# The token axis of a two-layer trunk kernel: 304 columns in the order meta, sample, prompt, and 288 where the meta tokens are dropped

## The chip, the cores and the metric

The kernel runs on one core of one Trainium2 chip. The metric is device microseconds of one execution, as the median of several runs. The engines of the core work side by side and in their own order: TensorE (PE, with its weight loads as PEld), VectorE (DVE), ScalarE (ACT), GpSimd (POOL) and SyncE (SP), which issues most DMAs.

## What is computed

One step of a trunk of two layers, for a prompt group (256 tokens, with 16 meta tokens ahead of them) and a sample group (8 sequences of 4 tokens) with the same weights. Layer 0 mixes with RWKV-7, layer 1 with Mamba-2; after each comes a PEER mixer, in which every token picks 16 of 16384 experts in each of 8 heads. The model width is 1024. The reference, cut:

```python
hp = concatenate([meta, x_prompt], axis=1)              # 16 + 256 tokens
yp, ... = trunk(hp, zeros..., lead_pad=M_CHUNK - N_META, chunk=M_CHUNK)
ys, ... = trunk(x_sample, states..., 0, x_sample.shape[1])
return (yp[:, N_META:], ys, ...)                        # states too

def trunk(h, ...):
    for i in range(DEPTH):                               # DEPTH = 2
        xn = rms_norm(h, norm_mix[i])
        out = rwkv7_time_mix(xn, ...) if i % 2 == 0 else mamba2_mix(xn, ...)
        h = h + out
        h = h + peer_ffn(rms_norm(h, norm_ffn[i]), ...)
    return rms_norm(h, norm_final), ...

# rwkv7, per head, one step of the scan
S = S * w_t + (S @ -kk_t) (kk_t * a_t)^T + v_t k_t^T
o_t = S @ r_t
# mamba2
zxbcdt = xn @ in_proj                                    # gate z, conv input x/B/C, dt
xbc = silu(conv_b + sum(full[:, j:j + L] * conv_w[j] for j in range(4)))   # causal, over tokens
y = ssd(...) + d_skip * xs                               # chunked state-space scan
yg = y * silu(z); yg = yg * rsqrt(mean(yg * yg) + eps) * norm_w            # per group of 512
out = yg @ out_proj
# peer
s = q . sub_keys; top 16 of 128 on both sides, then top 16 of their sums
out = sum over experts of gate * gelu(x . u_e) * v_e
```

The output of the meta tokens is not returned. They reach the prompt through the two mixers alone (the RWKV state, the conv and the Mamba state), so behind Mamba's projections nothing needs their columns any more.

## The kernel before

**Layout.** The residual `h` is held transposed: 128 partitions, 8 blocks of channels, and along the row the tokens, `T = 320` columns: 32 sample tokens, 16 meta tokens, 16 columns of zeros, 256 prompt tokens (`prep`). All elementwise work and most products have this token axis as their row, so they are 320 columns wide.

**Products.** `mm3` (L302, L303, L305) multiplies in three passes, for 8 blocks of the contraction: the weight's high part by the activation's high part (L302) and low part (L303), then the weight's low part by the high part (L305). That is 24 matmuls for one block of 128 output channels. The weights come by DMA as `wraw` (L287), ACT rounds them into `whi` (L276), and DVE or POOL makes `wlo` (L283, L281). Smaller products stay in plain fp32, which the trace shows as two instructions each.

**Stages, in order of time.**

- *RWKV front* (`rwkv`, 0 to 97 us): norm; the shifted difference `dx` (L378 to L383; POOL writes the columns where a sequence begins and clears the empty ones); LoRA products (L407, L408, L431, L432); then eight blocks of the key product `pk` by `mm3` with the gates (L451 to L458) between them.
- *RWKV heads* (`rwkv_heads`, 97 to 390 us): eight pairs of heads, each a generator, started nine ticks apart and advanced in turn. Each projects r and v (L607, fp32, 320 columns), scans the decay, and then works on five groups of 64 columns (`u` 0 to 4): group 0 holds samples, meta and the empty columns, groups 1 to 4 the prompt. Masks (`const_masks`) separate the sequences. The output is copied by one ACT instruction (L806), and the sample states are put in at the end (L811 to L835).
- *W_o* (390 to 426 us): eight blocks by `mm3` into `po`, added to `h`.
- *PEER 0* (`peer(0, 3)`, 426 to 1345 us): 16 query blocks `pq` by `mm3` (L892 evacuates them on DVE); scores of 64 + 128 + 128 tokens; the selection of the experts on DVE (`topk`), while PE begins with the first scan (`s_chunk`: 128 chunks of `psc`, 256 prompt columns each); one-hot products (L1120); and the second scan over the value table (L1273, `acc`), with the rest of the first scan woven in. The prompt goes through these dense scans; the samples and meta tokens are gathered row by row (L1051, L1148), in `ng = 3` groups of 16 columns.
- *Mamba* (`mamba`, 1345 to 1743 us): norm; 41 projection blocks `pi` by `mm3`: dt (block 40), 24 conv blocks (`conv`), 16 gate blocks z. A conv block is copied by ACT into `cst` (L1368 the samples, L1369 the rest); POOL fills in the old rows of the conv state, zeros, and a halo of three columns (L1370), which carries the last meta tokens across the empty columns to the prompt; ACT and three DVE instructions convolve (L1374, L1376), ACT applies Silu (L1379, L1381). Then per group of heads the state-space scan (`ssd`), the norm of the group (`pv`, L1581) and the output product `pout` (L1641 adds it to `h`).
- *PEER 1* (`peer(1, 2)`, 1743 to 2674 us): as PEER 0, but only samples and prompt are gathered and scanned; the query blocks still have all 320 columns. The final norm is at its end.

**Order.** Within a stage the order of the instructions on each engine is laid out when the kernel is built, by a planner that goes by priorities in the order of the code; in the two PEER stages (`tc.block(schedule_with_timeline_sim=True)`) it goes by a timeline of estimated durations as well. `keep_in_program_order` and `manual_schedule` fix some places by hand. DMAs of weights go through SP's queue, the gathers and the state outputs through POOL's.

Of the kernel before, what the change touches and what calls it, by code (L numbers as in the profile page):

```python
# [34 lines left out]
T = 320  # L35
D = 1024
# [34 lines left out]
def const_masks():  # L71
# [5 lines left out]
    chunk0 = np.where(t < 32, t // 4, np.where(t < 48, 100, 200 + t))  # L77
# [25 lines left out]
    for kb in range(8):  # L103
# [31 lines left out]
    c["sel0"] = ((np.where(p < 96, q, 32 + q))[:, None] == np.arange(64)[None, :]).astype(np.float32)  # L135
# [12 lines left out]
           "cr": ["mar", "ml1", "ml1t", "mx", "eye64", "blk", "hc", "hb", "rs", "mb", "mbq"],  # L148
# [77 lines left out]
class K:  # L226
    def __init__(self, ctx, tc, a, o):
# [9 lines left out]
        self.h = self.cp.tile([128, KB, T], F32, name="h")  # L237
# [103 lines left out]
    def rwkv(self):  # L341
# [34 lines left out]
        def shifted(k):  # L376

            V.scalar_tensor_tensor(xn[:, k], self.h[:, k], self.vec("nm0", k), ri, op0=ALU.mult, op1=ALU.mult)  # L378
            V.tensor_sub(dx[:, k, 1:], xn[:, k, :T - 1], xn[:, k, 1:])
# [94 lines left out]
        P.tensor_copy(sho[:, :, 0:8], xn[:, :, 3:32:4])  # L474
# [18 lines left out]
        def sm2(name, shape=(128, T), dt=F32):  # L493
            n = int(np.prod(shape[1:]))
            return sp.tile(list(shape), dt, name=name, tag=f"s{n}", bufs=SMB[n])
# [94 lines left out]
    def rwkv_heads(self, kb, xr, xv, kr, sgw, aa, inv2, oo, bv, sm, cm):  # L590
# [44 lines left out]
        for lo, hi, n in ((0, 32, 4), (32, 64, 16), (64, T, 64)):  # L635
# [10 lines left out]
        nc.gpsimd.tensor_copy(lamE[:, 0:8], lam[:, 3:32:4])  # L646
        nc.gpsimd.tensor_copy(lamE[:, 8:12], lam[:, 127:T:64])
# [13 lines left out]
        kEt = sm("kEt"); vt = sm("vt")  # L661
        kEt, vt = u5(kEt), u5(vt)
# [13 lines left out]
        pa5 = pab[:, 0:T].rearrange("p (u c) -> p u c", c=64)  # L676
        for u in U:
            ts = slice(u * 64, (u + 1) * 64)
            for hs in HS:
                mm(pab[hs, T:448] if u == 0 else pb4[hs, u - 1], lhsT=bh[hs, ts], rhs=ar[hs, :, ts], start=True, stop=True)  # L680
                mm(pa5[hs, u], lhsT=ar[hs, 0, ts], rhs=bh[hs, ts], start=True, stop=True)
        V.tensor_mul(X3[:, 0, 64:192], pab[:, T:448], mar[:, 0])
        V.tensor_mul(X3[:, 1:5, 64:192], pb4, mar[:, 1:2].to_broadcast([128, 4, 128]))
        Tm = u5(sm("Tm"))
        V.tensor_mul(Tm[:, 0], pa5[:, 0], C["ml1"][:, 0])
        V.tensor_mul(Tm[:, 1:5], pa5[:, 1:5], C["ml1"][:, 1:2].to_broadcast([128, 4, 64]))
        AT = u5(sm("AT"))
# [5 lines left out]
        for u in U:  # L693
            ts = slice(u * 64, (u + 1) * 64)
# [5 lines left out]
        TT = u5(sm("TT"))  # L700
        V.tensor_mul(TT, AT, C["ml1t"][:, None, :].to_broadcast([128, 5, 64]))
        TF = u5(sm("TF"))
        for li, sz in enumerate((2, 4, 8, 16, 32)):
# [8 lines left out]
            Xs = u5(sm("Xs"))  # L712
# [48 lines left out]
        nc.scalar.copy(QP[:, 0:32], pu0[:, 1, 0:32])  # L761
# [15 lines left out]
        V.tensor_add(QP[:, 32:64], pq0[:, 0:32], ar[:, 1, 0:32])  # L777
        V.tensor_add(QT, pq4[:, :, 64:128], u5(ar[:, 1, 64:T]))
# [27 lines left out]
        nc.scalar.copy(o, po.rearrange("p u c -> p (u c)"))  # L806
# [893 lines left out]
```

## Time and profile before

| what | value |
|---|---|
| median of 3 runs | 2676.23 us (2675.41 to 2686.91) |
| the profiled execution | 2676.22 us, span 2674.4 us |
| mean granted clock of TensorE | 0.977 |
| idle-free stages of PE | 97 to 390 us and 795 to 1320 us: 290.0 of 293 and 518.0 of 525 us busy |
| stretches with little PE work | 610 to 650 us (15.8 of 40 us), 1345 to 1420 us (50.9 of 75 us) |
| HBM traffic | 440.90 MB read, 16.69 MB written |

How such a page is read: the span runs from the first instruction to the last of one execution; what lies around it (1.8 us here) is not in the trace. An engine's busy share is a mean over stages that have different limits, so the windows view, which gives the busy time of each engine in a stretch, says more: where one engine fills a stretch, work taken off it shortens the stretch, and where none does, the waits say what each engine waited for. A matmul's shown duration holds the time until its result is out, and the next one starts before that; the time from start to start is what a matmul costs in a dense run of them.

### The profile page before, as it was taken

What the parts mean: (1) busy time and instruction counts of PE and PEld (TensorE: products, weight loads), DVE (VectorE), ACT (ScalarE), POOL (GpSimd) and SP (SyncE); (2) the same over time, 40 slices, a digit from 0 to 9 for tenths busy, and PEclk for the clock granted to TensorE, in tenths of its full rate; (3) what the DMA queues carried; (4) which work ended last, traced back from release to release, by engine and by line L of the source; (5) the groups of instructions that cost most, each with busy time, mean ns of one, the idle gap of its engine ahead of it and who ended that gap; (6) DMA issues with size and microseconds to landing.
All of it is one profiled execution on the core that took longest, in us unless ns stands there. A gap on an engine that the chain in (4) does not pass through costs nothing. (4 is left out here: it accounts for less than half of the span.)

```text
span 2674.4 us, 47364 instructions
## 1 busy us (share of the span) xinstructions
PE 2506.7 (94%) x18281; PEld 2156.3 (81%) x18281; DVE 1912.9 (72%) x3713; ACT 1246.7 (47%) x2324; POOL 1012.7 (38%) x895
## 2 busy tenths in 40 slices
PE   7999999996989999999978888999979899999998
PEld 4677769996978888888765776899979788888886
DVE  5355556897695777788784787769949856776777
ACT  3322233453784444444454543335448744444444
POOL 4111110485980233424146455106959501122220
PEclk9999999998999999999999999999989999999999
DMA  3111115453417788888732443454633267788784
GB/s 148 52 46 44 41 58 174 138 179 105 136 42 213 255 304 303 299 301 311 256 93 87 146 154 124 129 181 148 184 110 114 62 217 250 259 279 260 262 270 156
DMA packets 125858, 460.68 MB, mean 172 GB/s; under 512 B 14816, under 2 KB 15744, under 8 KB 122432
## 3 DMA queue, kind: packets, MB, share of 16 engines
q1 hardware_dynamic: 99488, 361.08, 42.0%
q0 software_dynamic: 26144, 96.56, 10.1%
q8 instruction: 144, 2.36, 0.4%
q14 instruction: 82, 0.67, 0.1%
HBM read 440.90 MB, written 16.69 MB: 171 GB/s over the span
## 5 line engine op out<-in xcount | busy, mean ns | idle before, releaser
L276 ACT CAST whi<-wraw 128x1024 fp32r<-128x1024 f32 (+1 forms) x619 | 641.9, 1038 | 892.0 <-PE acc L1273 283.5
L283 DVE TENSOR_TENSOR wlo<-wraw,whi 128x1024 fp32r<-128x1024 f32 (+1 forms) x493 | 601.2, 1220 | 423.8 <-ACT whi L276 326.9
L302 PE MATMUL psc<-xh,whi 128*128 128x256 f32 x2048 | 509.0, 285 | 4.6 <-ACT h L1065 2.6
L303 PE MATMUL psc<-xl,whi 128*128 128x256 f32 x2048 | 507.0, 284 | 0.0
L281 POOL TENSOR_TENSOR wlo<-wraw,whi 128x1024 fp32r<-128x1024 f32 (+1 forms) x150 | 357.5, 2390 | 181.3 <-PE pq L305 72.5
L302 PEld LDWEIGHTS psc<-xh,whi 128*128 128x128 f32 x2048 | 392.8, 192 | 12.0 <-ACT whi L276 3.0
L303 PEld LDWEIGHTS psc<-xl,whi 128*128 128x128 f32 x2048 | 392.9, 192 | 5.6
L305 PE MATMUL psc<-xh,wlo 128*128 128x256 f32 x2048 | 291.6, 284 | 0.3 <-POOL wlo L281 0.3
L1051 POOL DMA_INDIRECT G<-in_un,gi x80 | 112.1, 1401 | 472.6 <-DVE glo L283 308.9
L1273 PE MATMUL acc<-whi,glo 128*128 128x512 f32 x1024 | 284.4, 398 | 6.7 <-DVE glo L283 6.7
L1273 PE MATMUL acc<-whi,gh 128*128 128x512 f32 x1024 | 284.6, 398 | 4.4 <-ACT whi L276 3.3
L1273 PE MATMUL acc<-wlo,gh 128*128 128x512 f32 x1024 | 281.8, 396 | 0.0
L305 PEld LDWEIGHTS psc<-xh,wlo 128*128 128x128 f32 x2048 | 265.2, 192 | 1.2 <-POOL wlo L281 0.7
L1273 PEld LDWEIGHTS acc<-whi,glo 128*128 128x128 f32 x1024 | 193.3, 189 | 54.6 <-DVE glo L283 7.6
L1148 POOL DMA_INDIRECT G<-in_v,gi x80 | 120.1, 1502 | 302.7 <-DVE G L1143 165.7
L1273 PEld LDWEIGHTS acc<-wlo,gh 128*128 128x128 f32 x1024 | 192.7, 189 | 47.8 <-DVE wlo L283 1.3
L1273 PEld LDWEIGHTS acc<-whi,gh 128*128 128x128 f32 x1024 | 184.0, 189 | 44.8 <-ACT whi L276 6.5
L1120 PE MATMUL pwt<-ob,oa 128*128 128x128 f32 x1024 | 144.7, 281 | 11.6 <-DVE ob L1094 8.0
L1120 PEld LDWEIGHTS pwt<-ob,oa 128*128 128x128 f32 x1024 | 127.7, 191 | 23.1 <-issue 19.2
L302 PE MATMUL pi<-xh,whi 128*128 128x320 f32 x328 | 107.0, 337 | 13.1 <-ACT cst L1369 4.7
L303 PE MATMUL pi<-xl,whi 128*128 128x320 f32 x328 | 105.8, 334 | 4.1 <-DVE xl L336 3.8
L283 DVE TENSOR_TENSOR glo<-G,gh 128x256 fp32r<-128x256 f32 x256 | 106.7, 418 | 2.7 <-ACT gh L276 2.7
(485 smaller groups left out, 4462.4 us busy)
## 6 DMA issues: line engine op xcount, KB each, us to landing
wraw<-in_u SPq DMA_DIRECT2D x256, 512.0 KB
wraw<-in_v SPq DMA_DIRECT2D x256, 512.0 KB
wraw<-in_win SPq DMA_DIRECT2D x41, 512.0 KB
wraw<-in_wq SPq DMA_DIRECT2D x32, 512.0 KB
wraw<-in_rkv SPq DMA_DIRECT2D x24, 512.0 KB
h<-in_ssm SPq DMA_DIRECT2D x8, 1024.0 KB
out_sssm<-h POOLq DMA_DIRECT2D x8, 1024.0 KB, 4.7
wraw<-in_wo SPq DMA_DIRECT2D x8, 512.0 KB
```

Source lines behind the costliest of these rows:

```text
L276: self.nc.scalar.copy(hi, x)
L281: self.nc.gpsimd.tensor_sub(lo[:, :n], x[:, :n], hi[:, :n].bitcast(F32))
L283: self.nc.vector.tensor_sub(lo[:, n:], x[:, n:], hi[:, n:].bitcast(F32))
L302: nc.tensor.matmul(ps, lhsT=whi[:, k], rhs=xhi[:, x0 + k], start=start and k == 0, stop=False)
L303: nc.tensor.matmul(ps, lhsT=whi[:, k], rhs=xlo[:, x0 + k], start=False, stop=False)
L305: nc.tensor.matmul(ps, lhsT=wlo[:, k], rhs=xhi[:, x0 + k], start=False, stop=stop and k == kb - 1)
L1051: nc.gpsimd.indirect_dma_start(out=rows, out_offset=None, in_=a[f"un{l}"], in_offset=bass.IndirectOffsetOnAxis(ap=gi[:, 0, g, m:m + 1], ax ...
L1120: mm(pw[:, j], lhsT=oa[:, j], rhs=ob[:, j], start=True, stop=True)
L1148: nc.gpsimd.indirect_dma_start(out=rows, out_offset=None, in_=vrows, in_offset=bass.IndirectOffsetOnAxis(ap=gi[:, 1, g, m:m + 1], axis=0))
L1273: mm(acc[i], lhsT=g[:, t0:t0 + 128], rhs=w[:, d0:d0 + 512], start=b == 0 and g is gh and w is vhf, stop=b == 127 and w is vlf)
```

## The change

The token axis has 304 columns: 16 meta tokens, 32 sample tokens, 256 prompt tokens, with no empty columns. So the meta tokens can be dropped by starting a view at column 16, and what is left is contiguous.

- All of RWKV, the PEER 0 queries, and Mamba's dt and conv blocks take 304 columns.
- Mamba's gate blocks, gate, group norm and output product, and the PEER 1 queries take 288 (`M0`, `TM`, `C0`).
- Heads: the five groups stay 64 wide; group 0 is columns 0 to 63, and so holds the first 16 prompt tokens too, which its masks leave out; groups 1 to 4 begin at column 48. The output copy becomes two instructions, the add into `QP` two.
- Conv: meta and prompt now follow each other in `cst`, so POOL's halo copy is gone; the copy out of PSUM has three pieces in place of two, the Silu of the second part two in place of one, and the convolution has 328 columns in place of 344.
- The shifted difference needs no clearing of empty columns. The first scan reads the prompt from column 48 of rows of 304, before from column 64 of rows of 320. `h` keeps its 2560 columns of memory (`hp`), because PEER uses it as scratch.

The diff, cut to its core (the masks and index changes that only follow the new order are left out):

```diff
-T = 320
+T = 304
+TP = 320
...
-    x = np.concatenate([I["x_sample"].reshape(32, D), I["meta_tokens"], np.zeros((16, D), np.float32),
-                        I["x_prompt"].reshape(256, D)], axis=0)
+    x = np.concatenate([I["meta_tokens"], I["x_sample"].reshape(32, D), I["x_prompt"].reshape(256, D)], axis=0)
...
-        self.h = self.cp.tile([128, KB, T], F32, name="h")
+        self.hp = self.cp.tile([128, KB * TP], F32, name="h")
+        self.h = self.hp[:, 0:KB * T].rearrange("p (k t) -> p k t", t=T)
...
-            P.tensor_sub(dx[:, k, 0:32:4], shift[:, k], xn[:, k, 0:32:4])
-            P.tensor_scalar(dx[:, k, 32:33], xn[:, k, 32:33], -1.0, None, op0=ALU.mult)
-            P.memset(dx[:, k, 48:64], 0.0)
-            P.tensor_sub(dx[:, k, 64:65], xn[:, k, 47:48], xn[:, k, 64:65])
+            P.tensor_scalar(dx[:, k, 0:1], xn[:, k, 0:1], -1.0, None, op0=ALU.mult)
+            P.tensor_sub(dx[:, k, 16:48:4], shift[:, k], xn[:, k, 16:48:4])
+            P.tensor_sub(dx[:, k, 48:49], xn[:, k, 15:16], xn[:, k, 48:49])
...
+        us_ = lambda u: slice(0, 64) if u == 0 else slice(64 * u - 16, 64 * u + 48)
...
-            ts = slice(u * 64, (u + 1) * 64)
+            ts = us_(u)
...
-        V.tensor_add(QP[:, 32:64], pq0[:, 0:32], ar[:, 1, 0:32])
+        V.tensor_add(QP[:, 48:64], pq0[:, 16:32], ar[:, 1, 16:32])
+        V.tensor_add(QP[:, 0:16], pq0[:, 32:48], ar[:, 1, 32:48])
...
-        nc.scalar.copy(o, po.rearrange("p u c -> p (u c)"))
+        pof = po.rearrange("p u c -> p (u c)")
+        nc.scalar.copy(o[:, 0:48], pof[:, 0:48])
+        nc.scalar.copy(o[:, 48:T], pof[:, 64:320])
...
+        C0 = 48 - 16 * ng
...
-            pq = self.bank([128, T], "pq", "so"[i % 2])
-            self.mm3(pq, w, (xh, xl))
+            pq = self.bank([128, T - C0], "pq", "so"[i % 2])
+            self.mm3(pq, w, (xh[:, :, C0:], xl[:, :, C0:]))
...
-        TS = ((0, 64), (64, 192), (192, 320))
+        TS = ((C0, C0 + 64), (48, 176), (176, 304))
...
-            self.mm3(p, w, (xh[:, :, 64:T], xl[:, :, 64:T]))
+            self.mm3(p, w, (xh[:, :, 48:T], xl[:, :, 48:T]))
...
-        hs = self.h.rearrange("p k t -> p (k t)")
+        hs = self.hp
...
+        M0 = 16
+        TM = T - M0
...
-            p = self.bank([128, T], "pi", "i" if done[0] % NU < 2 or done[0] >= NU else "f")
+            c0 = M0 if blk < 16 else 0
+            p = self.bank([128, T - c0], "pi", "i" if done[0] % NU < 2 or done[0] >= NU else "f")
...
-            self.mm3(p, w, (xh, xl))
+            self.mm3(p, w, (xh[:, :, c0:], xl[:, :, c0:]))
...
-            if done[0] <= NU:
-                V.tensor_mul(s8[:, :, 3:7], p[:, 0:32].rearrange("p (b t) -> p b t", t=4), ri[:, 0:32].rearrange("p (b t) -> p b t", t=4))
-                V.tensor_mul(s[:, 59:347], p[:, 32:320], ri[:, 32:320])
-            else:
-                nc.scalar.copy(s8[:, :, 3:7], p[:, 0:32].rearrange("p (b t) -> p b t", t=4))
-                nc.scalar.copy(s[:, 59:347], p[:, 32:320])
-            P.tensor_copy(s[:, 88:91], s[:, 72:75])
+            for dst, src in ((s8[:, :, 3:7], slice(16, 48)), (s[:, 59:75], slice(0, 16)), (s[:, 75:331], slice(48, T))):
+                f = (lambda t: t.rearrange("p (b t) -> p b t", t=4)) if src.start == 16 else lambda t: t
+                if done[0] <= NU:
+                    V.tensor_mul(dst, f(p[:, src]), f(ri[:, src]))
+                else:
+                    nc.scalar.copy(dst, f(p[:, src]))
...
-            nc.scalar.activation(ac, s[:, 0:344], AF.Identity, bias=self.vec("cb", blk), scale=self.vec("cw", blk))
+            nc.scalar.activation(ac, s[:, 0:328], AF.Identity, bias=self.vec("cb", blk), scale=self.vec("cw", blk))
...
-            nc.scalar.activation(r[:, 96:384], ac[:, 56:344], AF.Silu)
+            nc.scalar.activation(r[:, 96:128], ac[:, 56:88], AF.Silu)
+            nc.scalar.activation(r[:, 128:384], ac[:, 72:328], AF.Silu)
...
-            pv = self.bank([128, T], "pv", "t")
+            pv = self.bank([128, TM], "pv", "t")
...
-            zs = gp.tile([128, 4, T], F32, name="zs", tag="zs")
+            zs = gp.tile([128, 4, TM], F32, name="zs", tag="zs")
...
-            p = self.bank([128, T], "pout", "i")
+            p = self.bank([128, TM], "pout", "i")
...
-            V.tensor_add(self.h[:, m], self.h[:, m], p)
+            V.tensor_add(self.h[:, m, M0:], self.h[:, m, M0:], p)
```

More of the change, by code (lines that the diff above doesn't have):

```diff
@@ L76, in const_masks @@
     t = np.arange(64)
-    chunk0 = np.where(t < 32, t // 4, np.where(t < 48, 100, 200 + t))
+    chunk0 = np.where(t < 16, 100, np.where(t < 48, t // 4, 200 + t))
     mar = np.zeros((128, 2, 2, 64), np.float32)
@@ L134, in const_masks @@
     c["rs3"] = rs3
-    c["sel0"] = ((np.where(p < 96, q, 32 + q))[:, None] == np.arange(64)[None, :]).astype(np.float32)
+    c["sel0"] = ((p[:, None] < 96) & (q[:, None] == np.arange(32)[None, :])).astype(np.float32)
     c["bmask"] = (q[:, None] // 4 == np.arange(8)[None, :]).astype(np.float32)
@@ L494, in sm2 @@
             n = int(np.prod(shape[1:]))
-            return sp.tile(list(shape), dt, name=name, tag=f"s{n}", bufs=SMB[n])
+            w = n // T * TP if n % T == 0 else n
+            t = sp.tile([128, w], dt, name=name, tag=f"s{w}", bufs=SMB[w])[:, 0:n]
+            return t if len(shape) == 2 else t.rearrange("p (a b) -> p a b", b=shape[2])
         self.psum(r=1, A=2, L=2, c=2, s=1)
@@ L595, in tr, with sm5 @@
         def tr(pt, src, u, hs):
-            mm(pt[hs, u], lhsT=src[hs, u * 64:(u + 1) * 64], rhs=C["eye"][hs, hs], start=True, stop=True)
+            mm(pt[hs, u], lhsT=src[hs, us_(u)], rhs=C["eye"][hs, hs], start=True, stop=True)
         def u5(t):
             return t.rearrange("p (u c) -> p u c", c=64)
+        us_ = lambda u: slice(0, 64) if u == 0 else slice(64 * u - 16, 64 * u + 48)
+        def sm5(name):
+            return u5(sm(name, (128, 320)))
         v = sm("v")
@@ L634, in rwkv_heads @@
         dE = sm("dE")
-        for lo, hi, n in ((0, 32, 4), (32, 64, 16), (64, T, 64)):
+        for lo, hi, n in ((0, 16, 16), (16, 48, 4), (48, T, 64)):
             cv = cs[:, lo:hi].rearrange("p (c n) -> p c n", n=n)
@@ L760, in rwkv_heads @@
         nc.scalar.copy(PU[:, 0], pu0[:, 0])
-        nc.scalar.copy(QP[:, 0:32], pu0[:, 1, 0:32])
+        nc.scalar.copy(QP[:, 16:48], pu0[:, 1, 16:48])
         nc.scalar.copy(PU[:, 1:5], pu4)
@@ L819, in rwkv_heads @@
         for hs in HS:
-            mm(pst[hs], lhsT=PX[hs], rhs=C["eye64"][hs, 32:64], start=True, stop=True)
-        V.tensor_add(o[:, 0:32], o[:, 0:32], pst)
+            mm(pst[hs], lhsT=PX[hs], rhs=C["sq"][hs], start=True, stop=True)
+        V.tensor_add(o[:, 16:48], o[:, 16:48], pst)
         yield
@@ L891, in peer @@
         for i in range(16):
-            V.tensor_mul(qT[:, i], pq.pop() if i == 0 else query(i), ri)
+            V.tensor_mul(qT[:, i, C0:], pq.pop() if i == 0 else query(i), ri[:, C0:])
         for k in range(KB):
@@ L898, in peer @@
             for k in range(4):
-                mm(ptx[:, k * 128:(k + 1) * 128], lhsT=xn[:, half * 4 + k, 0:64], rhs=C["eye"], is_transpose=True, start=True, stop=True)
+                mm(ptx[:, k * 128:(k + 1) * 128], lhsT=xn[:, half * 4 + k, C0:C0 + 64], rhs=C["eye"], is_transpose=True, start=True, stop=True)
             nc.scalar.copy(xt[:, half * 512:half * 512 + 512], ptx)
         nc.gpsimd.dma_start(xd, xt)
-        TS = ((0, 64), (64, 192), (192, 320))
+        TS = ((C0, C0 + 64), (48, 176), (176, 304))
         sc = {}
@@ L1168, in gather @@
                         for k in range(4):
[L1169 removed]
+                            mm(ph[32 * g:32 * g + 16, k * 128:k * 128 + 128], lhsT=self.h[:, 4 * half + k, C0 + 16 * g:C0 + 16 * g + 16],
                                rhs=C["eye"], start=True, stop=True)
@@ L1359, in conv @@
             p = proj(16 + blk)
-            s = gp.tile([128, 347], F32, name="cst", tag="cst", bufs=3)
+            s = gp.tile([128, 331], F32, name="cst", tag="cst", bufs=3)
             s8 = s[:, 0:56].rearrange("p (b t) -> p b t", t=7)
@@ L1575, in ssd @@
             nc.gpsimd.dma_start(self.o["pssm"][g], S)
-            pv = self.bank([128, T], "pv", "t")
+            pv = self.bank([128, TM], "pv", "t")
             for j in range(4):
-                sq = gp.tile([128, T], F32, name="gsq", tag="cst", bufs=3)
+                sq = gp.tile([128, TM], F32, name="gsq", tag="cst", bufs=3)
                 nc.scalar.activation(sq, yg[:, j], AF.Square)
                 mm(pv, lhsT=C["ones"], rhs=sq, start=j == 0, stop=j == 3)
-            r = gp.tile([128, T], F32, name="gr", tag="cst", bufs=3); ri = gp.tile([128, T], F32, name="gri", tag="cst", bufs=3)
+            r = gp.tile([128, TM], F32, name="gr", tag="cst", bufs=3); ri = gp.tile([128, TM], F32, name="gri", tag="cst", bufs=3)
             nc.scalar.activation(r, pv, AF.Sqrt, bias=C["cst"][:, 0:1], scale=1.0 / 512)
```

68 lines of the change are left out of this document (33 added, 35 removed).

## The prediction

> **What bounds the kernel now.** I read the page first, then the windows view cut at the borders of the stages, then the groups by shape, and the timeline where an engine waits.
>
> ```profile
> span 2674.4 us, 47364 instructions
> ...
> PE 2506.7 (94%) x18281; PEld 2156.3 (81%) x18281; DVE 1912.9 (72%) x3713; ACT 1246.7 (47%) x2324; POOL 1012.7 (38%) x895
> ```
>
> TensorE (PE) is busy for 94% of the span. Ends of matmuls are modelled, so this share alone proves nothing; the stages decide. Columns of the next fence: the window, its length, the busy us of PE, PE weight loads, DVE, ACT and POOL with their counts, the granted clock, the DMA share, GB/s.
>
> ```profile
> 0.00:42.00 42.00, 25.99 (x69) 11.72 (x69) 29.00 (x50) 13.46 (x24) 22.10 (x56) 1.00 0.51 197
> 42.00:97.00 55.00, 52.39 (x271) 36.03 (x270) 6.17 (x14) 25.43 (x50) 16.23 (x6) 1.00 0.19 59
> 97.00:390.00 293.00, 290.02 (x4457) 207.81 (x4458) 167.92 (x396) 76.28 (x189) 43.69 (x70) 1.00 0.15 49
> 390.00:426.00 36.00, 33.82 (x203) 28.18 (x202) 21.33 (x34) 11.65 (x18) 5.55 (x5) 1.00 0.30 99
> 426.00:488.00 62.00, 60.17 (x396) 57.92 (x397) 36.42 (x54) 21.70 (x28) 2.97 (x2) 1.00 0.55 178
> 488.00:682.00 194.00, 169.06 (x1395) 167.04 (x1394) 164.53 (x580) 91.87 (x145) 136.62 (x58) 0.94 0.47 145
> 682.00:1345.00 663.00, 648.88 (x3860) 564.98 (x3858) 506.62 (x795) 354.53 (x662) 253.63 (x213) 0.99 0.72 242
> 1345.00:1420.00 75.00, 50.87 (x263) 42.60 (x262) 68.03 (x103) 40.87 (x89) 41.24 (x56) 0.88 0.27 82
> 1420.00:1648.00 228.00, 203.04 (x1152) 166.76 (x1151) 154.40 (x179) 109.84 (x238) 118.82 (x166) 0.94 0.36 123
> 1648.00:1743.00 95.00, 90.49 (x556) 78.92 (x556) 68.72 (x100) 30.68 (x49) 24.90 (x25) 0.98 0.48 155
> 1743.00:1807.00 64.00, 60.62 (x382) 58.49 (x383) 39.20 (x53) 20.64 (x28) 5.39 (x4) 0.95 0.57 179
> 1807.00:2665.00 858.00, 821.34 (x5294) 735.89 (x5292) 644.51 (x1347) 449.27 (x809) 341.56 (x237) 0.98 0.62 199
> ```
>
> In order: LoRA, key product, RWKV heads, W_o, queries of PEER 0, its selection, its two scans; Mamba's start, body and output; queries of PEER 1, all the rest of it. PE ends last in most stages. The start of Mamba is DVE's (68 of 75 us), and its body has about 25 us in which PE waits. The selection and the scans (two thirds of the span) work on 256 prompt columns and 64 gathered rows before and after, so the change can act on some 950 us (0 to 488 and 1345 to 1807).
>
> **What a column costs.** The first fence is the chain of waits (start, length, what); the second is the timeline of Mamba's output product, twelve matmuls from its first row to its last.
>
> ```profile
> 2131.87 0.96 PE psc L305 x8
> 2132.82 5.60 PE acc L1273 x24
> ```
>
> ```profile
> 1736.89 0.31 PE L302 MATMUL pout<-hl,whi 128*128 128x320 f32 x1
> ...
> 1738.65 0.31 PE L302 MATMUL pout<-hl,whi 128*128 128x320 f32 x1
> ```
>
> From start to start: 0.95/8 = 119 ns at 256 columns, 1.76/12 = 146.7 ns at 320, 5.60/24 = 233 ns at 512. Between 256 and 320 that is 0.43 ns per column, up to 512 it is 0.45; 288 and 304 lie between measured points. So 16 columns fewer save 6.8 ns, 32 fewer 13.7 ns.
>
> Against this stands the Trainium skill, "TensorE: Matmul & The Clock Gate", section "Back-to-back issue gap": a sustained stream of loads and matmuls is put at 81 ns for 128 columns and 131 ns for 512. That slope is 0.13 ns per column, and by it the three-pass products would save about 8 us. The 233 ns above contradict it; I go by the trace.
>
> Products in plain fp32 run as two instructions each:
>
> ```profile
> L607 PE MATMUL pr<-xr,wraw x128: 432/432/537, 99.2 to 299.1; 128*128 128x320 f32 x128
> L607 PE MATMUL pr<-xv,wraw x128: 432/432/537, 108.9 to 368.6; 128*128 128x320 f32 x128
> L916 PE MATMUL pss<-G x192: 270/275/324, 488.1 to 1821.2; 128*128 128x128 f32 x128, 128*64 128x128 f32 x64
> ```
>
> (432 - 270)/192 = 0.84 ns per column, 13.5 ns an instruction for 16 columns.
>
> **The change part by part.** The counts of the three-pass products (`mm3`; L303 and L305 have the same count as L302):
>
> ```profile
> L302 PE MATMUL pi<-xh,whi 128*128 128x320 f32 x328 | 107.0, 337 | 13.1 <-ACT cst L1369 4.7 <-ACT xh L276 3.6 <-ACT whi L276 3.1
> L302 PE MATMUL pq<-xh,whi 128*128 128x320 f32 x256 | 78.5, 319 | 1.3 <-DVE h L1641 0.7 <-DVE h L586 0.7
> L302 PE MATMUL pout<-hl,whi 128*128 128x320 f32 x128 | 40.5, 328 | 0.0
> L1581 PE MATMUL pv<-gsq,c 128*128 128x320 f32 x32 | 10.7, 457 | 2.0 <-ACT gsq L1580 1.9
> ```
>
> - LoRA stage: 64 fp32 instructions x 13.5 ns = 0.9 us, but PE has 26 of 42 us; about 0.6 with the shorter vector work and eight small memsets less on POOL.
> - Key product: 8 blocks x 24 = 192 x 6.8 = 1.3; fp32 beside it (gates, norms) fills 64 slots x 13.5 = 0.9. PE has 52 of 55 us: **2.2**.
> - Heads: r and v 256 instructions, five helpers of 16 each, 336 x 13.5 = 4.5. The chunk products stay five groups of 64 (group 0 now overlaps the first prompt tokens, masked), so "no padding" saves nothing there. A second output copy on ACT and a second small add on DVE per head lie beside PE, which has 290 of 293 us; if that cover went they would cost some 0.2 us each, 3 us in all. I take 80%: **3.6**.
> - W_o: 192 x 6.8 = 1.3, less a little: **1.2**.
> - PEER 0 queries: half of pq, 384 x 6.8 = **2.6**. The next bound is DVE in the selection; it starts on the scores, so it moves forward by the same.
> - PEER 1 queries, 288 columns: 384 x 13.7 = 5.3, and its first blocks run at a lower clock (0.95 over the stage): **5.5**.
> - Mamba: 25 of the 41 pi blocks (conv, dt) at 304: 600 x 6.8 = 4.1; 16 gate blocks at 288: 384 x 13.7 = 5.3; pout 384 x 13.7 = 5.3; pv 32 x 27 = 0.9; 15.6 in all. Seven conv blocks (168 x 6.8 = 1.1) lie in the start that is DVE's; there 30 vector operations with 16 columns less give 0.5, at (477 - 411)/64 = 1.0 ns per column by the two rows below. Of the other 14.5 I take 85%, since PE has 293.5 of 323 us: 12.3.
>
> ```profile
> L892 DVE TENSOR_TENSOR G<-pq,G x32: 477/491/492, 445.9 to 1809.3; 128x320 f32<-128x320 f32 x32
> L1237 DVE TENSOR_TENSOR G<-G,h x124: 411/418/422, 802.7 to 2621.5; 128x256 f32<-128x256 f32 x124
> L379 DVE TENSOR_TENSOR dx<-xn x8: 477/484/585, 14.2 to 35.5; 128x319 f32<-128x319 f32 x8
> ```
>
> Mamba also loses the POOL copy of the conv's halo, on which ACT waits, and gains one ACT copy and one Silu per block (rows: waits; one line's durations min/median/max; timeline; a window):
>
> ```profile
> ACT ac L1374 <- POOL cst L1370: 31.6, 20, 4.5
> PE pg L1534 <- POOL co L1371: 10.3, 2, 5.3
> ```
>
> ```profile
> L1370 POOL COPY cst<-cst x24: 178/186/1181, 1371.9 to 1620.4; 128x3 f32<-128x3 f32 x24
> L1531 DVE TENSOR_TENSOR G<-E,cb x24: 677/683/4564, 1452.5 to 1702.5; 128x512 f32<-128x512 f32 x24
> L1368 ACT COPY cst<-pi x21: 167/180/192, 1380.2 to 1616.8; 128x32 f32<-128x32 f32 x21
> L1379 ACT ACTIVATE xc<-ac x72: 213/217/235, 1379.5 to 1630.6; 128x32 f32<-128x32 f32 x72
> ```
>
> ```profile
> 1537.58 4.56 DVE L1531 TENSOR_TENSOR G<-E,cb 128x512 f32<-128x512 f32 x1
> ...
> 1542.29 1.94 PE L1534 MATMUL pg<-xdt,G 128*128 128x64 f32 x8 [5.32 <-POOL co L1371]
> ...
> 1543.36 0.67 ACT L1374 ACTIVATE ac<-cst,vecs 128x344 f32<-128x344 f32 x1 [4.50 <-POOL cst L1370]
> ```
>
> ```profile
> 1530.00:1550.00 20.00, 14.59 (x81) 11.98 (x80) 19.30 (x15) 9.08 (x20) 15.17 (x24) 0.83 0.06 12
> ```
>
> ACT gets 24 x (0.18 + 0.22) = 9.6 us more at most; it has 110 of 228 us, so I cost it at nothing, and at 9.6 if PE came to wait for all of it. ACT's wait for POOL goes (31.6 us, 20 times). What is late next is DVE: PE waited 5.32 us for an operation of L1531 that took 4.56 us instead of 0.68 while POOL ran. The view puts this wait down to POOL's L1371, but L1531 ended last (1542.14). Bounds for the relief: 0, and both PE waits of this kind, 10.3 us. As the long DVE operation itself is not touched, I take 2. Mamba: 12.3 + 0.5 + 2 = **14.8**.
>
> Sum: 0.6 + 2.2 + 3.6 + 1.2 + 2.6 + 14.8 + 5.5 = 30.5. The profiled execution took 2676.2 us (span 2674.4), the same as the median of the runs, 2676.2; so 2645.7, forecast **2646** (2638 to 2654).
>
> **The rivals.**
> - *The vector side paces Mamba and the heads* (0.17). PE's savings then become longer waits. For it: DVE at 68 of 75 us and the 5.32 us wait; against it: long stretches of the body with no wait on PE at all. If a third of Mamba's 15.6 is left and nothing in the heads: 0.6 + 2.2 + 1.2 + 2.6 + 5.2 + 5.5 = 17.3, **2659**. The clock (0.94 in the body) would go down with longer waits. The Trainium skill, on the same page, section "Part 1: The HAM clock gate", gives half clock after an idle window of about 3.4 us and full clock after a busy one; an estimate by that rule is 1.7 us more (half of a window) for each new wait of that length. Around the wait above the trace agrees, at 0.83.
> - *The halo's removal opens both long waits* (0.12): all 10.3 instead of 2, and with each the clock of 0.83 over 20 us, 0.17 x 20 = 3.4 us, of which I count half: 8.3 + 3.4 more, **2634**.
> - *The planner's order turns out worse* (0.09). Orders on the engines are laid out from estimated durations that all change a little. One more wait such as the 25 us by which PE's 169 us fall short of the 194 in PEER 0's selection, 20 of it not given back: **2666**, within 0.5%.
> - *Where operands start* (0.05), the case that ends slower. The columns of xh move from rows of 1280 bytes to rows of 1216, and the first scan reads from column 48, not 64: 3 x 2048 psc matmuls. No row shows PE on such an address. The selections hide up to 25 us each, or 9 ns on each of their 2688 matmuls (2 x 56 chunks x 24); the other 3456 are bare, so 9 ns more per matmul eats all 30.5 us, and a tenth of the pitch (12 ns) gives 41 + 8 - 30.5 = 19 us lost: **2695**. Against it: L379 reads with a shift of 4 bytes, and DVE's 477 ns are those of L892.
> - *The slope is flatter than 0.43* (0.01): only a third of the 25 us of `mm3` terms, **2663**; the three pitches speak against it.
>
> **How the numbers follow.** Forecast 0.56, rivals 0.17, 0.12, 0.09, 0.05, 0.01. The range 2632 to 2662 holds the first three; out of it lie the last three and some of the edges, under 2 in 10. A measurement can tell 0.5% (13.4 us) from no change. Faster by more (below 2662.8): 0.56 + 0.12 + most of 0.17 = 0.83; within: 0.11; slower by more: 0.06.
>
> **What would show it.** The start-to-start time of `mm3` rows is 140 ns at 304 and 133 at 288, and psc stays at 119. The stretch of query blocks is 2.6 us shorter in PEER 0 and 5.5 in PEER 1, Mamba (1345 to 1743) 15 us shorter, heads 3 to 4. The L1370 wait of ACT is gone, and PE's wait for L1531 stays. I would be wrong if psc's pitch moved, if Mamba lost under 8 us, or if a scan stage changed its length by more than 3 us.

## The result and the profile after

The change makes the kernel faster: 2634.36 us (median of four runs, 2628.68 to 2636.73) against 2675.82 on the same chip (2674.05 to 2686.91), a ratio of 0.983 with the interval 0.9813 to 0.9847. By this ratio the 2676.23 us from before become 2630.7, which lies just below the range of 2632 to 2662. The gain is some 45 us by the ratio and by the profiles below (41.5 by the two medians), where 30.5 were forecast.

The profiled execution took 2634.19 us. First the page's span and busy times, then the windows view at the borders of the stages, with the columns of the prediction's fence:

```profile
span 2632.3 us, 47459 instructions
...
PE 2477.9 (94%) x18281; PEld 2137.4 (81%) x18281; DVE 1898.8 (72%) x3724; ACT 1253.6 (48%) x2384; POOL 1008.2 (38%) x863
```

```profile
0.00:38.90 38.90, 24.34 (x69) 11.57 (x69) 26.86 (x47) 11.88 (x22) 20.62 (x48) 1.00 0.55 211
38.90:99.60 60.70, 55.62 (x274) 38.25 (x273) 7.32 (x18) 28.10 (x54) 16.39 (x6) 0.91 0.16 54
99.60:392.40 292.80, 290.51 (x4479) 212.06 (x4480) 168.84 (x407) 72.95 (x193) 43.69 (x71) 0.99 0.15 49
392.40:423.30 30.90, 28.61 (x180) 24.38 (x176) 18.86 (x30) 11.66 (x19) 4.98 (x4) 1.00 0.37 114
423.30:483.00 59.70, 57.75 (x397) 55.35 (x398) 35.61 (x53) 21.54 (x28) 2.95 (x2) 1.00 0.58 184
483.00:669.30 186.30, 166.26 (x1392) 165.18 (x1392) 157.46 (x580) 91.97 (x145) 135.46 (x58) 0.95 0.49 151
669.30:1331.80 662.50, 648.78 (x3870) 565.98 (x3868) 511.60 (x799) 357.29 (x665) 255.82 (x215) 0.99 0.71 242
1331.80:1400.00 68.20, 48.90 (x253) 42.30 (x254) 63.61 (x101) 39.50 (x95) 36.37 (x48) 0.85 0.28 87
1400.00:1617.70 217.70, 197.01 (x1159) 161.19 (x1159) 155.12 (x180) 118.45 (x282) 123.01 (x148) 0.94 0.39 132
1617.70:1708.30 90.60, 85.29 (x549) 74.52 (x549) 65.90 (x99) 29.80 (x48) 24.66 (x25) 0.96 0.48 157
1708.30:1770.40 62.10, 57.44 (x397) 54.22 (x398) 38.28 (x53) 21.44 (x29) 6.60 (x4) 0.97 0.58 185
```

PE fills the same stages as before. Several rows surprise. The second one, the key product, has a granted clock of 0.91 where before had 1.00. The sixth, PEER 0's selection, lost 7 us of DVE's busy time with the same 580 instructions. And the two Mamba rows behind the start lost 14.7 us, more than the 12.3 that the columns were to give.

Both kernels were profiled a second time, unchanged. The table gives the length of each stage in both profiles, between starts of matmuls in the timeline: the first `pr`, the last `pns`, the first `pq`, `pss` and `pwt`; a scan from its first to its last `acc`, Mamba from its first `pi` to its last `pout`. The stretches between these, of which the two from the first `pwt` to the first `acc` (some 116 us each) are the longest, moved by under 0.5 us and are left out. The gain is the difference of the two means.

| stage | forecast gain | before | after | gain |
|---|---|---|---|---|
| LoRA and key product | 2.8 | 99.2, 101.3 | 99.6, 98.0 | 1.4 |
| heads | 3.6 | 294.6, 294.6 | 292.8, 291.2 | 2.6 |
| W_o | 1.2 | 32.4, 35.4 | 30.9, 30.9 | 3.0 |
| queries 0 | 2.6 | 61.9, 61.9 | 59.6, 60.2 | 2.0 |
| selection 0 | 0 | 193.7, 193.7 | 186.3, 186.9 | 7.1 |
| scan 0 with the value table | 0 | 546.2, 548.1 | 542.7, 545.1 | 3.3 |
| Mamba | 14.8 | 394.2, 395.8 | 375.6, 376.1 | 19.1 |
| queries 1 | 5.5 | 66.1, 65.7 | 62.1, 61.5 | 4.1 |
| selection 1 | 0 | 190.4, 190.5 | 189.2, 189.5 | 1.1 |
| scan 1 with the value table | 0 | 547.9, 546.0 | 545.8, 545.6 | 1.2 |
| whole span | 30.5 | 2674.4, 2680.8 | 2632.3, 2633.6 | 44.7 |

A column costs what the prediction said. Timeline of after: products of 304 columns in the key product, then of 288 in the output product.

```profile
39.11 0.30 PE L306 MATMUL pk<-xlo,whi 128*128 128x304 f32 x1
...
41.08 0.30 PE L306 MATMUL pk<-xlo,whi 128*128 128x304 f32 x1
```

```profile
1705.92 0.29 PE L305 MATMUL pout<-hl,whi 128*128 128x288 f32 x1
...
1706.85 0.29 PE L306 MATMUL pout<-hl,whi 128*128 128x288 f32 x1
```

1.97/14 = 141 ns at 304 and 0.93/7 = 133 ns at 288; 140 and 133 were expected. So the question is what else moved: 12.7 us in the selections and scans, which were to stay as they were, and 4.3 us too much in Mamba.

### The profile page after: what moved, and what is told of

Read it like the earlier page. It is cut to its first block, busy times and chain, and to the rows that moved or that the text cites. A ratio compares the mean times of both kernels' runs of the same rounds, so it can differ in the third digit from the quotient of the medians.

```text
span 2632.3 us, 47459 instructions
## 1 busy us (share of the span) xinstructions
PE 2477.9 (94%) x18281; PEld 2137.4 (81%) x18281; DVE 1898.8 (72%) x3724; ACT 1253.6 (48%) x2384; POOL 1008.2 (38%) x863
## 3 DMA queue, kind: packets, MB, share of 16 engines
q0 software_dynamic: 26144, 96.56, 10.2%
## 5 line engine op out<-in xcount | busy, mean ns | idle before, releaser
L286 DVE TENSOR_TENSOR wlo<-wraw,whi 128x1024 fp32r<-128x1024 f32 (+1 forms) x493 | 593.7, 1204 | 397.2 <-ACT whi L279 339.6
L305 PE MATMUL pi<-xh,whi 128*128 128x304 f32 (+1 forms) x328 | 102.5, 331 | 11.7 <-ACT xh L279 3.7
L279 ACT CAST gh<-G 128x256 fp32r<-128x256 f32 x256 | 101.8, 399 | 11.7 <-PE acc L1288 11.6
```

Source lines behind the costliest of these rows:

```text
L279: self.nc.scalar.copy(hi, x)
L286: self.nc.vector.tensor_sub(lo[:, n:], x[:, n:], hi[:, n:].bitcast(F32))
L305: nc.tensor.matmul(ps, lhsT=whi[:, k], rhs=xhi[:, x0 + k], start=start and k == 0, stop=False)
```

## The experiments

**Both kernels once more.** No edit.

> The changed kernel once more, unaltered, to part what belongs to the kernel from what belongs to one execution. Theory (phase): of the 42 us that the profiled executions differ by, about 30 are columns, and the rest lies in times that depend on how two engines happen to meet: the selection of PEER 0 (12.5 us of lead at its end, 5.1 at its start: 7.4 us without any instruction less), the scans (3.4 and 2.1 us), less a half-clock stretch of 10.2 us in the key product. Then the selection, the scans or that stretch come out otherwise by 2 to 7 us here, while query blocks and key product repeat within 0.5 us; the time lies between 2626 and 2638. Rival (systematic): the new placement of the columns makes these stages shorter for good; then the selection of PEER 0 takes 186.3 us again, within 1 us, and the second scan 542.7.

> The kernel before, unchanged, in a second profiled execution. Theory: the 193.6 us of PEER 0's selection (first pss to first pwt) belong to this kernel, because POOL's wlo instructions meet short DVE operations at the same places in every execution: 192 to 195 us again, against 186 to 187.3 in the five profiles with 304 columns. Rival (one execution's luck): 186 to 190, and then about 6 us of the profiled difference between the two kernels are no effect of the change. Scan 0 (546.2) and scan 1 (547.9) are expected within 2 us of these values; the front without a stretch of half clock before the first head product.

after_again took 2632.32 us (2628.49 to 2635.49; before on that chip 2679.62), ratio 0.9817 (0.9795 to 0.9839). The stages are in the table. The selection repeats within 1 us in both kernels, so its length is no accident of one execution; after_again's theory (phase), by which it would come out otherwise, missed, and before_again's theory held, but for a front 2 us longer, with a clock of 0.96 in LoRA, where full clock was expected. Scan 0 of after, 542.7, was partly an accident. The W_o of before was 3 us longer in the second profile, which makes its mean gain too large.

**What carries Mamba's gain.** wide_320 takes the columns back in Mamba's three-pass products (`xh`, `xl` and `hl` are 320 wide, zeros behind the tokens), keep_304 gives the 16 meta columns back to its gate and output products and to PEER 1's queries, halo_back puts a POOL copy where the halo copy was (onto itself, so that its wait returns).

```diff
 # wide_320
-        xh = pp.tile([128, KB, T], F32R, name="xh")
+        xhw = pp.tile([128, KB, 320], F32R, name="xh")
...
-            self.mm3(p, w, (xh[:, :, c0:], xl[:, :, c0:]))
+            self.mm3(p, w, (xhw, xlw))
 # keep_304
-            self.mm3(pq, w, (xh[:, :, C0:], xl[:, :, C0:]))
+            self.mm3(pq, w, (xh, xl))
...
-        M0 = 16
+        M0 = 0
 # halo_back
+            P.tensor_copy(s[:, 72:75], s[:, 72:75])
             P.tensor_copy(co[:, blk, 0:8], s8[:, :, 4:7])
```

> The kernel after, but in Mamba all products by three passes (projections and output) run over 320 columns again, with columns of zeros behind the 304 or 288; everything else (copies, convolution without halo, gates and norms of 288) as after. Left out of nothing that counts in the result. Theory A (columns carry Mamba's gain): 600 x 6.8 + 768 x 13.7 = 14.6 us of PE come back, of which 85% show: Mamba 375.6 + 12.4 = 388 us, and 6 us stay gained from the halo, the shorter vector operations and the order. Theory B (as a column given back at 304 brought only 2.4 to 2.9 of 7.9 us, the columns carry a third of the gain): Mamba 380 to 383.

> The new order of tokens without the dropping of the meta tokens: Mamba's gate blocks, gate, group norm and output product and the PEER 1 queries take 304 columns in place of 288 (the meta columns of h behind Mamba are then filled with values that nothing uses). By the slope of 0.43 ns a column, 6.8 ns for each of 1152 matmuls is 7.9 us, pv 0.4 us: about 8 us slower than the changed kernel if PE paces these stages (Mamba 5.5, PEER 1 queries 2.6), 2642. If the vector side paces Mamba, under 5 us in all (2639); if the slope is that of a third, 3 us.

> The changed kernel with a POOL copy of three columns onto themselves in each conv block, where the halo copy was, so that ACT's first conv instruction waits for POOL again. My forecast put this wait at 2 us of Mamba's time: 2636. Rival: it is all of PE's two long waits, 10 us and a half-clock stretch: 2645. If Mamba's extra 3.7 us over the forecast come from the planner's other order, Mamba's length moves by some us either way, and ACT's wait for POOL is back at 20 to 30 us without showing in the time.

wide_320: 2647.42 us, ratio 0.9885 (0.9869 to 0.9902), Mamba 389.5 us. Windows of Mamba as the table bounds it, in before, after and wide_320:

```profile
1347.87:1742.05 394.18, 342.64 (x1957) 287.37 (x1957) 287.82 (x374) 179.14 (x371) 184.17 (x245) 0.94 0.37 124
```

```profile
1331.80:1707.40 375.60, 330.93 (x1957) 277.95 (x1957) 284.05 (x377) 187.34 (x423) 183.91 (x221) 0.93 0.39 129
```

```profile
1334.00:1723.50 389.50, 339.17 (x1956) 284.82 (x1957) 290.23 (x377) 180.34 (x417) 171.26 (x225) 0.93 0.37 125
```

13.6 us come back (389.5 - 375.9), as theory A had it: the columns carry most of Mamba's gain. The rows call for some caution. From before to after PE's busy time fell by 11.7 us and the rest of the stage, in which PE stands idle, by 6.9 (51.5 to 44.7). In wide_320 8.2 us of busy time come back and 5.7 of idle time, because PE waits longer for the long DVE operations there (20.6 us, last fence below). So the 13.6 us are not the columns' work alone. The split is rough: PE's busy time also differs by some 4 us between two profiles of one kernel.

keep_304: 2635.68 us, 0.9829 (0.9807 to 0.9851); Mamba 378.4 and queries 1 63.7 us, 2.6 and 1.9 more than the means of after, where 384 x 2 x 6.8 = 5.2 and 2.6 were worked out. That is under the 5 us in all by which its expectation marks the rival that the vector side paces Mamba. But Mamba took 371.8 to 377.9 us in the seven profiles of kernels that have it as in after, so 2.6 us can't be told from the scatter; wide_320, with more columns, speaks against that rival.

halo_back: 2634.19 us, 0.9833 (0.981 to 0.9856), Mamba 377.2, inside that scatter: no gain from the halo is shown, and the rival that opens both long waits falls. The waits views of before, after, halo_back and wide_320:

```profile
ACT xc L1379 <- DVE ac L1376: 25.0, 15, 3.8
```

```profile
ACT xc L1397 <- DVE ac L1394: 31.5, 12, 6.3
PE pg L1554 <- DVE G L1551: 5.9, 3, 2.9
```

```profile
ACT ac L1393 <- POOL cst L1389: 25.9, 14, 5.7
PE pg L1555 <- DVE G L1552: 3.1, 2, 2.8
```

```profile
PE pg L1557 <- DVE G L1554: 20.6, 4, 9.7
```

ACT's wait for POOL's halo copy, 31.6 us, is gone in after, and ACT waits 6.5 us more for DVE's convolution instead; in halo_back the wait for POOL is back with 25.9 us, and the time hardly changes. PE's wait behind the long DVE operations went from 10.3 to 5.9 us, and the seven profiles have 5.8 or 5.9. As it is 3.1 in halo_back, the missing halo copy is not what shortened it. Narrower vector operations and the order, which the planner laid out anew, are candidates, but no run takes them apart.

**Is the selection of PEER 0 shorter because of the columns?** In it short DVE operations meet POOL's `wlo` instructions. One such place in the timeline of before, DVE and then POOL, and the durations of that line (minimum, median, maximum) in before and in after:

```profile
513.92 1.75 DVE L968 TENSOR_TENSOR G<-G 128x8 f32<-128x8 f32 x1
```

```profile
513.25 2.40 POOL L281 TENSOR_TENSOR wlo<-wraw,whi 128x1024 fp32r<-128x1024 f32 x1 [0.40 <-ACT whi L276]
```

```profile
L968 DVE TENSOR_TENSOR G<-G x24: 157/398/2447, 510.2 to 598.4; 128x16 f32<-128x16 f32 x7, 128x32 f32<-128x32 f32 x3, 128x8 f32<-128x8 f32 x3, 128x64 f32<-128x64 f32 x3
```

```profile
L983 DVE TENSOR_TENSOR G<-G x24: 155/195/2430, 505.0 to 584.8; 128x16 f32<-128x16 f32 x7, 128x32 f32<-128x32 f32 x3, 128x8 f32<-128x8 f32 x3, 128x64 f32<-128x64 f32 x3
```

The DVE operation, 0.16 us at its shortest, ends with POOL's at 515.66. Each meeting costs up to 2.3 us, and in after fewer operations of this line are hit: its median fell from 398 to 195 ns. The Trainium skill, "SBUF — State Buffer", section "SBUF: two separate sides", tells of a port pair that VectorE and GpSimd share as an exclusive lock, held for a whole instruction. The two rows agree: 513.92 + 1.75 and 513.25 + 2.40 are 515.67 and 515.65.

Five kernels shift the two against each other: 18 more matmuls in the last query block (both kernels), which move the whole selection against the transfers, and 3 or 8 more ahead of the first scan's first chunk, which move PE and `wlo` against DVE.

```diff
 # before_q18, after_q18
+            for _ in range(18 if l == 0 and i == 15 else 0):
+                mm(pq, lhsT=w[0][:, 0], rhs=xh[:, 0], start=True, stop=True)
 # phase_8, before_phase_3, before_phase_8: n = 8, 3, 8 (in phase_8 the columns are 48:T)
+            for _ in range(n if l == 0 and b == 0 else 0):
+                mm(p, lhsT=w[0][:, 0], rhs=xh[:, 0, 64:T], start=True, stop=True)
```

> The kernel before with 18 more matmuls in the last query block of PEER 0 (their result is overwritten by the block's own first matmul), 18 x 146.7 ns = 2.6 us, so that the selection starts that much later against the transfers of its weights. Theory A (where POOL's wlo instructions meet the short DVE operations is a matter of phase): the queries are 2.6 us longer and the selection changes its length by a step of 2 to 7 us, as each meeting costs about 2 us. Theory B (the selection is shorter for another reason that the column count brings): it stays within 1 us of the kernel before.

> The kernel after with 18 more matmuls in the last query block of PEER 0 (their result is overwritten by the block's own first matmul), 18 x 140 ns = 2.5 us, which restores the length of that stage before the change. Theory A (phase): PEER 0's selection goes back from 186.3 towards 193.6 us, 190 or more. Theory B: it stays at 186 to 187.5.

> The kernel after with 8 more matmuls ahead of the first scan's first chunk in both PEER stages (overwritten by the chunk's own first matmul): 8 x 119 ns = 0.95 us by which PE and the wlo instructions that follow it are later against the selection's DVE operations. Theory P (the length of the selection hangs on where in their period of 2.86 us the wlo instructions meet DVE): the selection of PEER 0 moves by 2 us or more, to either side of 186.3. Theory Q (the shorter period alone makes it shorter): it stays within 1 us.

> The kernel before with 3 more matmuls ahead of the first scan's first chunk in PEER 0 (overwritten by the chunk's own first matmul): 3 x 120 ns = 0.36 us of shift between PE, with the wlo instructions behind it, and the selection's DVE operations; the planner lays the order of these out anew. Theory P (193.6 us is one unlucky layout among several of this kernel, within some tenths of a microsecond): the selection of PEER 0 comes to 185 to 191. Theory S (320 columns make it long in a systematic way): 192 to 195 again.

> As before_phase_3 with 8 more matmuls, 0.96 us of shift. Theory P: 185 to 191 us for the selection of PEER 0, and not the same as with 3. Theory S: 192 to 195.

| kernel | selection 0 | time of one run |
|---|---|---|
| before, before_again, before_q18 | 193.7, 193.7, 193.3 | 2680.81 (before_q18) |
| before_phase_3 | 188.8 | 2675.67 |
| before_phase_8 | 191.0 | 2677.94 |
| after, after_again, after_q18 | 186.3, 186.9, 186.2 | 2631.41 (after_q18) |
| phase_8 | 186.4 | 2628.77 |

Windows of the selection in before_phase_3, then in before_phase_8:

```profile
491.00:680.00 189.00, 168.99 (x1396) 168.05 (x1395) 156.51 (x580) 92.60 (x145) 135.58 (x57) 0.94 0.48 148
```

```profile
490.00:681.00 191.00, 168.41 (x1400) 167.32 (x1399) 161.88 (x580) 92.20 (x145) 136.44 (x57) 0.94 0.49 147
```

The shift of the transfers does nothing: theory B held in before_q18 and after_q18. In before_phase_3, with 320 columns, the selection is 5 us shorter and DVE is busy 8 us less (164.53 to 156.51, 580 instructions each); in before_phase_8 it is 3 us shorter. Theory P held in both, theory S falls: part of the 193.7 us belongs to the layout of the kernel before, the same in every execution, and not to its columns. In the whole time little of this is seen (2675.67 us, one run, against 2677.59), as W_o was 3 us longer in that profile. phase_8 stayed at 186.4 us, as theory Q had it, so not every shift matters.

These edits change two things at once, since the planner also laid DVE's instructions out in another order: in the timeline 206 of the 580 places differ from before in before_phase_3, and 247 in before_phase_8. before_start_48 and row_1280, below, keep DVE's order and change only PE's pitch. They took 191.7 us (before 193.7) and 189.0 (after 186.3). So timing alone moves the selection by 2 to 3 us, to either side. Between before and after, DVE's order differs at 63 places, all among the first 134. The first L968 starts 22 us into the selection in both (510.2 - 488.1 and 505.0 - 483.0), the last 110.3 and 101.8 us into it; most of the lead arises where the order is the same.

What stays open is how much of the 7 us the columns bring. No kernel whose token axis has 320 columns came under 188.8 us, and the eleven profiles of kernels with 304 lie between 186.1 and 189.0.

**The place from which a matmul reads.** The wlo pass (eight matmuls) of consecutive chunks of the first scan, in PEER 0's selection, in before and in after:

```profile
534.91 1.12 PE L305 MATMUL psc<-xh,wlo 128*128 128x256 f32 x8
537.79 1.12 PE L305 MATMUL psc<-xh,wlo 128*128 128x256 f32 x8
```

```profile
520.82 1.11 PE L308 MATMUL psc<-xh,wlo 128*128 128x256 f32 x8
523.67 1.11 PE L308 MATMUL psc<-xh,wlo 128*128 128x256 f32 x8
```

2.88/24 = 120 ns against 2.85/24 = 119 ns, for the same 256 columns: psc's pitch did move. Three kernels take its two causes apart, the length of a row of `xh` and `xl` (1280 bytes before, 1216 after) and the column at which psc begins to read (64 before, 48 after). The edits are in both PEER stages, for `xl` as for `xh`.

```diff
 # row_1280
-        xh = gp.tile([128, KB, T], F32R, name="xh")
+        xh = gp.tile([128, KB, TP], F32R, name="xh")[:, :, 0:T]
 # start_64
+        xh = gp.tile([128, KB, TP], F32R, name="xh")[:, :, 16:TP]
 # before_start_48 (the kernel before)
+        xh = gp.tile([128, KB * T + 64], F32R, name="xh")[:, 48:48 + KB * T].rearrange("p (k t) -> p k t", t=T)
```

> The kernel after, but in both PEER stages the rows of xh and xl are 1280 bytes apart again, as before the change; the columns begin at the row's start as after (the first scan reads from column 48). Theory A (the distance of the rows sets the pitch of psc, which the second profiles show at 119.0 ns after against 119.9 before): 119.9 again, the chunk period 2.88 us instead of 2.855, scans 1.5 to 2 us longer each (547), and PEER 0's selection back at 192 to 194 us, as the meetings on the shared port follow this period. Theory B (the column at which the read begins, 48 instead of 64, does it): 119.0, selection 186 to 187.

> As row_1280, and the columns begin 16 further into the row, so that the first scan reads from column 64 of rows of 1280 bytes, exactly as before the change; all products keep 304 and 288 columns. Theories A and B both give psc at 119.9 ns, scans of 547 us and a selection of 192 to 194 us in PEER 0. Rival C (neither; the other tiles or the order do it): 119.0 ns and 186 to 187 us.

> The kernel before with 320 columns and rows of 1280 bytes, but the tiles xh and xl of both PEER stages begin 48 columns further, so that the first scan reads from column 112, which lies in its 256 bytes where column 48 lies (192 bytes in). Theory A (where the read begins within 256 bytes sets the pitch of psc, 0 bytes slow, 192 bytes fast): psc at 113 to 114 ns instead of 119.9, as in row_1280; scan 1 at 540 to 542 us instead of 546 to 548. Theory B (the pitch hangs on the 304 columns or the tile's size): 119.9 and 546 to 548.

The wlo pass in scan 1, in before, in row_1280 and in before_start_48:

```profile
2131.71 1.12 PE L305 MATMUL psc<-xh,wlo 128*128 128x256 f32 x8
2140.17 1.12 PE L305 MATMUL psc<-xh,wlo 128*128 128x256 f32 x8
```

```profile
2093.34 1.07 PE L308 MATMUL psc<-xh,wlo 128*128 128x256 f32 x8
2101.69 1.07 PE L308 MATMUL psc<-xh,wlo 128*128 128x256 f32 x8
```

```profile
2127.30 1.07 PE L305 MATMUL psc<-xh,wlo 128*128 128x256 f32 x8
2135.64 1.07 PE L305 MATMUL psc<-xh,wlo 128*128 128x256 f32 x8
```

With 0.28 us for the last one, seven starts take 0.84 us in the first fence (120 ns) and 0.79 in the other two (113 ns); a round of psc and `acc` takes 8.46 against 8.35 and 8.34 us.

| kernel | row, first column read | median pitch of psc | scan 0, scan 1 | selection 0 |
|---|---|---|---|---|
| before | 1280 B, 64 | 120 | 546.2, 547.9 | 193.7 |
| after | 1216 B, 48 | 118 (mean 119) | 542.7, 545.8 | 186.3 |
| start_64 | 1280 B, 64 | 120 | 543.9, 546.9 | 187.3 |
| row_1280 | 1280 B, 48 | 113 | 542.9, 539.7 | 189.0 |
| before_start_48 | 1280 B, 112 | 114 | 541.0, 541.1 | 191.7 |

Both theories on row_1280 missed: neither 119.9 nor 119.0, but 113. The place decides: reads from column 48 and from 112, which lie 256 bytes apart, are fast, those from 64, between them, are slow. With rows of 1216 bytes the eight blocks lie at different places within 256 bytes, and after has a mixture: the medians of the seven starts in its wlo pass run from 116 to 126 ns. Counted from the start of the tile, the first and the fifth block lie where all eight lie in row_1280, and they are not the fast ones, so the whole rule is not shown. before_start_48 settles that the place counts, as theory A had it: 320 columns and rows as before, the reads moved alone, and both scans are 5 to 7 us shorter, the whole 2665.12 us in one run (before 2677.59). start_64 has before's pitch, as expected, but a selection of 187.3 us where 192 to 194 were expected, and a first scan of 543.9 where 547 was: the pitch does not make the selection. row_1280 as a whole took 2630.78 us, start_64 2643.24, one run each.

**The clock in the key product, and the best pieces together.** In after, PE waits for ACT in the first round of the key product, and a stretch of half clock follows (timeline, then windows):

```profile
44.39 0.87 PE L475 MATMUL pn<-ks,cr 128*16 128x304 f32 x2 [1.90 <-ACT ks L474]
```

```profile
45.30:55.50 10.20, 10.20 (x34) 7.59 (x36) 0.86 (x2) 2.46 (x5) 3.06 (x1) 0.52 0.16 51
```

In the nine profiles of kernels that leave this stage as in after, the wait is 1.70 to 1.91 us. Behind the longer ones, of 1.90 and 1.91, stand some 7 to 10 us of half clock; in wide_320 (1.70) and in phase_8 (1.76, next line) none.

```profile
44.66 0.69 PE L475 MATMUL pn<-ks,cr 128*16 128x304 f32 x2 [1.76 <-ACT ks L474]
```

pn_late issues that matmul a block later. best is pn_late with rows of 1280 bytes in both PEER stages and in Mamba.

```diff
 # pn_late
+            if k:
+                mm(pn, lhsT=C["hc"][:, k - 1], rhs=ks, start=k == 1, stop=False)
...
-            mm(pn, lhsT=C["hc"][:, k], rhs=ks, start=k == 0, stop=k == KB - 1)
+        mm(pn, lhsT=C["hc"][:, KB - 1], rhs=ks, start=False, stop=True)
```

> The changed kernel with each norm product pn of the key product issued after the gates of the block, so that PE does not wait 1.9 us for ACT's square of the first block. In the profiled execution of the changed kernel TensorE's clock was halved for 10.2 us right behind that wait, 5.1 us lost; before, the wait was 0.94 us and no half clock followed. If that wait is the cause, the wait falls under 0.8 us, the half-clock stretch is gone and the heads begin 5 to 6 us earlier: 2628. If the half clock comes from elsewhere, the time stays within 2 us of the changed kernel.

> pn_late and row_1280 together, and rows of 1280 bytes for xh and xl in Mamba as well. If the pieces add up: front 6 to 8 us shorter than after, 2 to 3 of them given back later; scans 2 and 6 us shorter, selection 0 some 2.5 longer; Mamba as after (375), or 3 to 6 us shorter if the pitch of its 304-column products goes from 139.5 to 134 ns. Altogether 2617 to 2626 us, ratio to before 0.977 to 0.981; no gain over pn_late (0.9804) if PE's saving in the scans turns into waits.

pn_late keeps the full clock, as its window of the key product shows:

```profile
38.60:91.10 52.50, 50.54 (x274) 35.00 (x273) 7.37 (x18) 27.99 (x54) 16.45 (x6) 1.00 0.18 62
```

52.5 us instead of 60.7, and the heads begin 7 to 8 us earlier, where 5 to 6 were expected. In that profile all of it was given back later (queries 62.4, scan 0 546.5, Mamba 377.9; span 2633.2 us against 2632.3 and 2633.6). It took 2629.18 us, ratio 0.9804 (0.978 to 0.9828), beside after_again's 2632.32 and 0.9817; the intervals overlap, so a gain over after is not shown. best took 2625.32 us (2621.59 to 2632.15, before 2677.59), ratio 0.9812 (0.9796 to 0.9829). Its scans are shorter (539.6 and 540.4), its selections longer (188.9 and 194.5), and Mamba's pitch at 304 columns stayed at 140 ns. It beats the kernel before; the interval of its ratio overlaps with that of after, so a gain over after is not shown here either.

## Why the prediction was right and where it failed

- **Right:** the direction, and PE's price per column: 141 and 133 ns; Mamba's columns brought PE 11.7 us of busy time and 13.6 us by wide_320, where the sum had 12.3. The flatter slope of the Trainium skill, "TensorE: Matmul & The Clock Gate", section "Back-to-back issue gap", does not hold for these products. Heads 2.6 (3.6 forecast), queries 2.0 and 4.1 (2.6 and 5.5) and W_o 1.5 by the undisturbed profile (1.2) were sized within some 1.5 us.
- **The step that failed** is in the first part: "The selection and the scans (two thirds of the span) work on 256 prompt columns and 64 gathered rows before and after, so the change can act on some 950 us". The operations are the same, but not what they meet and not where they read. The sum put nothing for these stages, and they gained 12.7 us, most of the 14 that it lacked: 7.1 in PEER 0's selection, where short DVE operations meet POOL's `wlo` at other moments (up to 5 us of this is shown to be layout, the rest is open), 3.3 and 1.2 in the scans, 1.1 in the other selection. Without the 7.1 us the time would have been inside the range. The prediction had named the sign, "if a scan stage changed its length by more than 3 us", but no rival for it.
- **The rival on where operands start** named the right place and the wrong direction. The prediction said "I would be wrong if psc's pitch moved"; it moved by 1 ns downward, which is 72 x 0.03 = 2 us in each scan, about what the scans show. start_64, which gives the pitch back, does not separate it from the scatter of the scans.
- **Mamba was mis-sized**: 19.1 instead of 14.8. The columns came out as forecast; the term of 2 us for PE's relief from waits was too small, as PE's idle time fell by 6.9 us, at least 4.4 of them behind the long DVE operations. The halo was the wrong reason for it, and the right one is open. "Vector side paces" falls for the most part, as the gain was larger than forecast; keep_304 alone leaves a doubt.
- **The front** gave 1.4 of 2.8, and that this is near is luck. Two terms were off and offset each other: LoRA took 38.9 us in both profiles of after instead of 42.0 and 44.0 (first start of `pk`), 3 us or more where 0.6 was forecast, for a reason that no run shows; the key product took 60.7 and 59.1 us instead of 57.3, where 2.2 less was forecast. There the new order made a wait of 1.90 us, and pn_late shows that without it the half clock is gone. That is a small case of the planner rival.
- **The range** began 1.3 us too high, since the stages costed at nothing had no bounds of their own.

## What to carry to other kernels

Where two engines meet on a shared resource for hundreds of short operations, a stage's length depends on the layout: give it a range of several microseconds even where none of its operations changes, and shift the stage by some tenths of a microsecond before a difference is credited to a change. When a tile's row length or first column changes, measure the pitch of the matmuls that read it; here an offset of 48 columns was worth 5 to 7 us in each scan.

## What the runs showed of the hardware

- For the same 256 columns a matmul's pitch was 120 ns when its rows were read from the place of column 64 and 113 ns from that of column 48 or 112, in rows of 1280 bytes. Why is open.
- A wait of 1.90 us was followed by 10.2 us at a clock of 0.52, one of 1.76 us in another profile by no half clock. The Trainium skill, "TensorE: Matmul & The Clock Gate", section "Part 1: The HAM clock gate (the "warmup" mystery)", speaks of an idle window of about 3.4 us; here the wait was shorter, though it stands behind LoRA, in which PE is busy for 24 of 39 us, so other idle time may have counted.
